# Expert groups of a two-layer trunk: two announced blocks per group, a down product in quarters, and VectorE and ScalarE in program order

## Chip, cores and metric

The kernel runs on one core of a Trainium2 chip. The metric is the device time of one execution in microseconds (us). Before the change three runs took 1015.21, 1004.9 and 1011.58 us; the median is 1011.58 us.

## What is computed

Two layers of a decoder trunk on 256 tokens of width 1024. Each layer has a token mixer, a cross-attention and a mixture of experts, with a layer norm behind each. The change lies in the experts alone:

```python
g_idx = jnp.argmax(g_logits, axis=-1)                      # one of 8 groups per token
e_logits = e_logits[jnp.arange(s), g_idx]
top_val, top_idx = lax.top_k(e_logits, TOP_K_IN_GROUP)     # 2 of the group's 4 experts
top_w = jax.nn.softmax(top_val, axis=-1) * g_weight
...
hid = jax.nn.silu(jnp.einsum('sd,edf->sef', xs, w_gate)) * jnp.einsum('sd,edf->sef', xs, w_up)
return jnp.einsum('sef,efd->sd', hid * gates[:, :, None], w_down)
```

There are 32 experts of inner width 256, so each layer reads 96 MB of expert weights. How many tokens an expert gets is known only when the router has run.

## The kernel before

**Groups.** `moe` (one call per layer) serves the eight groups one after the other, in the order of `SERVED`: 0 to 7 in the first layer, 1, 3, 0, 2, 4, 5, 6, 7 in the second. `expert(g)` (line 1405) computes a group. The four experts of the group stand side by side in the 128 columns or rows of TensorE, 32 tokens each: one matmul per expert, with 32 stationary columns.

**The straight path** of a group handles the first 32 tokens of each expert. In this order: the gate product (`up_to(b, 0, xg, wg)`, 8 steps k of four matmuls each, 256 columns), `silu` on ScalarE, the second half of the down product's way back of the group before (`late_back`), the up product (`up_to(b, 1, xg, wu)`), `act` on VectorE (the product of both), then the gather of the next group's tokens into `xg` by two `gather_half` (8 matmuls each into one bank; half 0 is evicted by VectorE, half 1 by ScalarE, four instructions each, through `affine`, line 460 or 462), then `dispatch(g, 32)`, the selection matrix of the second block, and `turned` (two transposes and an eviction by ScalarE, line 427).

**Blocks.** Tokens beyond 32 go in blocks of 32 through `over` (line 1366): `If(rv > 32 * c)`, with the next block's test nested in it, for c from 1 to 7. `rv` is the group's largest count, read from `cnt` into a register at run time. A block (`whole`) gathers its own tokens into `xo`, does gate, up, turn and down with the same weights. The group in `SPREAD` (group 0, the third served of the second layer) does only gate and up in its nest (`part`), and the down products in a second nest (`rest`). Here two groups of the first layer (3 and 6) take block 1 and skip block 2; of the second layer, group 0 takes blocks 1 to 3 and skips block 4, and group 2 takes block 1 and skips block 2; all other groups skip block 1.

**Announcements.** `foresee(rv, n)` puts a register operation and a branch hint into TensorE's program and names a test that comes later. For block 1 it stands ahead of step `TELL` of the up product (3 in both layers, 6 or 8 in a layer's first group); for every block c from 2 on it stands in the block before, behind the first `rows` of its `down` (`between`), or at the start of the block in `part`.

**Down product.** `down` (line 1295): `rows(c, n)` multiplies the turned activations by the down weights, two steps f of four matmuls of 512 columns; ScalarE evicts them times the gate weight as the high part of `y` (line 1310), VectorE subtracts to get the low part (line 1311). `back(c, n, y)` brings the tokens back to their places with the matrix `dt` that `combine` made: four matmuls of 512 columns, added to `ff` by VectorE (line 1327). Both have two halves. Between them `begin(n)` reads the next group's count, makes its `dt` and gate weight (`combine`) and its selection matrix (`dispatch` into `dn`).

**Weights.** Each group's 12 weight tiles of 1 MB are loaded by SyncE's transfer queue in one fixed order, over tiles that `free` returns: the gate and up tiles behind the group's nest of blocks, the down tiles behind its straight down product. The queue runs ahead as far as tiles are free.

**Order.** The framework's scheduler orders each engine's instructions unless a `manual_schedule` names the engine. ScalarE is pinned to program order up to the nest of each group, VectorE only until the first group's nest (`pinned[1].close()`).

## Time and profile before

| | |
|---|---|
| runs | 1015.21, 1004.9, 1011.58 us; median 1011.58 us |
| profiled execution | 1013.67 us, its span 1011.9 us |
| TensorE busy | 923.1 us (91%), 7948 matmuls |
| VectorE busy | 503.3 us (50%) |
| ScalarE busy | 340.9 us (34%) |
| transfers | 272.59 MB, mean 269 GB/s |
| weights' queue (q1) | 68.2% of the span |

The expert stage of the first layer takes about 270 to 512 us, that of the second 758 to 1000 us. The shares above are means over stages with different limits, so the stages are read one by one in the rows below. A row of the chain, of waits or of the timeline names an engine, a line, and tiles as `out<-in`; "PEq", "ACTq" or "DVEq" is the engine's instruction stream itself (a branch, a register, a semaphore), and L1368 stands for the `If`. The matmuls of a step overlap (four of them run side by side in the row groups of TensorE), so a duration times a count is more than the busy time.

### The profile page before, as it was taken

How to read it: one execution, taken by the hardware profiler on the slowest of the kernel's cores; microseconds unless marked ns; L12 is line 12 of the kernel's file. 1: busy time of each engine (PE TensorE's matmuls, PEld its weight loads, DVE VectorE, ACT ScalarE, POOL GpSimd, SP SyncE). 2: the span in 40 equal slices, each digit the busy share in tenths (PEclk: the TensorE clock that was granted, in tenths of full speed). 3: DMA queues.
4: the chain of work that ended last, by engine and by line, in shares of the span. 5: the costliest groups of instructions: out<-in, count | busy, mean ns of one | idle time of the engine just before them, and what ended most of it. 6: DMA issues, size and time to landing. Idle time of an engine off the chain costs nothing. (4 is left out here: it accounts for less than half of the span.)

```text
span 1011.9 us, 19936 instructions
## 1 busy us (share of the span) xinstructions
PE 923.1 (91%) x7948; PEld 688.2 (68%) x7948; DVE 503.3 (50%) x1258; ACT 340.9 (34%) x736; POOL 0.2 (0%) x4
## 2 busy tenths in 40 slices
PE   7899999999998688989899999999999888997885
PEld 7888987898754354856368899789885564444541
DVE  5755755544653333323466575554465414644434
ACT  5454855343411121011144475435442121121111
POOL 0000000000000000000000000000000000000000
PEclk9999999999999899999999999999999999999998
DMA  9842334538769988999786244553784994719995
GB/s 351 343 147 99 134 128 161 209 125 331 293 268 422 424 348 367 424 425 420 250 336 229 108 147 180 174 208 110 288 351 196 421 387 183 318 58 421 422 363 203
DMA packets 43774, 272.59 MB, mean 269 GB/s; under 512 B 4832, under 2 KB 5344, under 8 KB 13280
## 3 DMA queue, kind: packets, MB, share of 16 engines
q1 hardware_dynamic: 43472, 270.26, 68.2%
q8 instruction: 86, 1.41, 0.5%
q14 instruction: 72, 0.59, 0.2%
q10 hardware_dynamic: 144, 0.33, 0.1%
HBM read 269.52 MB, written 1.05 MB: 267 GB/s over the span
## 5 line engine op out<-in xcount | busy, mean ns | idle before, releaser
L432 DVE SCALAR_TENSOR_TENSOR wl<-main,wh 128x1024 fp32r<-128x1024 f32 (+1 forms) x93 | 112.2, 1211 | 112.1 <-ACT wh L431 111.9
L431 ACT ACTIVATE wh<-main 128x1024 fp32r<-128x1024 f32 (+1 forms) x93 | 97.3, 1052 | 116.5 <-PE bank L438 68.3
L437 PE MATMUL bank<-xh,wh 128*128 128x256 f32 x368 | 108.8, 298 | 5.6 <-ACT xh L488 3.6
L438 PE MATMUL bank<-xl,wh 128*128 128x256 f32 x368 | 105.8, 288 | 1.0 <-DVE xl L432 0.6
L439 PE MATMUL bank<-xh,wl 128*128 128x256 f32 x368 | 104.9, 286 | 0.0
L1277 PE MATMUL bank<-ext,xg 128*32 128x256 f32 x912 | 88.2, 392 | 2.9 <-DMA ext<-exp 2.8
L1327 DVE TENSOR_TENSOR ff<-ff,bank 128x512 f32<-128x512 f32 x84 | 53.2, 681 | 49.9 <-PE bank L1322 49.9
L437 PEld LDWEIGHTS bank<-xh,wh 128*128 128x128 f32 x368 | 71.1, 194 | 7.0 <-ACT xh L488 4.1
L438 PEld LDWEIGHTS bank<-xl,wh 128*128 128x128 f32 x368 | 71.3, 194 | 2.2 <-DVE xl L432 0.9
L439 PEld LDWEIGHTS bank<-xh,wl 128*128 128x128 f32 x368 | 71.4, 194 | 0.1
L1277 PE MATMUL bank<-main,xg 128*32 128x256 f32 x640 | 66.1, 384 | 2.4 <-DMA main<-exp 2.4
L460 ACT ACTIVATE xg<-bank,prmb 128x128 f32<-128x128 f32 x64 | 24.0, 456 | 123.3 <-PE bank L1227 117.2
L1310 ACT ACTIVATE y<-bank,sm 128x512 fp32r<-128x512 f32 (+1 forms) x46 | 30.7, 669 | 103.5 <-PE bank L1306 76.1
L1322 PE MATMUL bank<-y,dt 128*128 128x512 f32 (+1 forms) x184 | 56.9, 422 | 7.9 <-DVE y L1311 7.2
L1306 PE MATMUL bank<-ext,dn 128*32 128x512 f32 (+1 forms) x212 | 46.6, 670 | 17.5 <-PEq L1368 6.8
L437 PE MATMUL bank<-wh,oh 128*128 128x512 f32 (+1 forms) x160 | 60.9, 380 | 0.0
L439 PE MATMUL bank<-wh,ol 128*128 128x512 f32 (+1 forms) x160 | 59.1, 369 | 0.0
L1322 PEld LDWEIGHTS bank<-y,dt 128*128 128x128 f32 x184 | 29.6, 188 | 43.2 <-ACT y L1310 16.4
L438 PE MATMUL bank<-wl,oh 128*128 128x512 f32 (+1 forms) x160 | 59.0, 369 | 0.0
L1277 PEld LDWEIGHTS bank<-ext,xg 128*32 128x32 f32 x912 | 42.6, 112 | 22.5 <-issue 4.7
L1227 PEld LDWEIGHTS bank<-dn,xhat 128*128 128x128 f32 x448 | 51.1, 192 | 5.8 <-issue 4.9
L1227 PE MATMUL bank<-dn,xhat 128*128 128x128 f32 x448 | 53.7, 278 | 0.0
(300 smaller groups left out, 2008.7 us busy)
## 6 DMA issues: line engine op xcount, KB each, us to landing
ext<-exp SPq DMA_DIRECT2D x75, 1024.0 KB, 16.6
main<-exp SPq DMA_DIRECT2D x54, 1024.0 KB, 12.8
main<-wsq SPq DMA_DIRECT2D x33, 1024.0 KB, 5.0
main<-win SPq DMA_DIRECT2D x22, 1024.0 KB, 6.8
M<-exp SPq DMA_DIRECT2D x17, 1024.0 KB, 15.0
VM<-exp SPq DMA_DIRECT2D x8, 1024.0 KB, 17.1
xx<-exp SPq DMA_DIRECT2D x7, 1024.0 KB, 14.0
M<-wsq SPq DMA_DIRECT2D x5, 1024.0 KB, 7.1
```

The costliest lines, as they stand in the source:

```text
L431: ACT.activation(hi, src, AF.Copy, scale=scale)
L432: DVE.scalar_tensor_tensor(lo, src, scale, hi.bitcast(F32), op0=ALU.mult, op1=ALU.subtract)
L437: PE.matmul(psum, lh, rh, start=first, stop=False, skip_group_check=True)
L438: PE.matmul(psum, lh, rl, start=False, stop=False, skip_group_check=True)
L439: PE.matmul(psum, ll, rh, start=False, stop=last, skip_group_check=True)
L460: ACT.activation(dst, src, AF.Identity, bias=b, scale=g)
L1227: PE.matmul(b[:, k * 128:(k + 1) * 128], xhat[:, t, c:c + 128], d[:, t], start=(t == 0 and k == 0), stop=(t == 1), skip_group_check=True)
L1277: PE.matmul(pg[m * i:m * i + m, which * S:(which + 1) * S], x[:, k, m * i:m * i + m], w[:, k], start=(k == 0), stop=(k == 7), skip_group_c ...
L1306: PE.matmul(b[m * i:m * i + m], ht[:, f * 128 + m * i:f * 128 + m * i + m], w[:, o:o + n], start=(f == 0), stop=(f == 1), skip_group_check ...
L1310: ACT.activation(hi, b, AF.Copy, scale=gate)
L1322: PE.matmul(bs[t], dt[:, t * 128:(t + 1) * 128], y[i], start=(i == 0 and not held), stop=(i == 1), skip_group_check=bool(held))
L1327: DVE.tensor_add(o, o, bs[t])
```

## The change

- `TELL` becomes (7, 14) in both layers. For the groups that are not a layer's first, the announcement of block 1 goes from step 3 of the up product to step 7 of the gate product; a layer's first group has it at step 6 of the up product (before: 6 in the first layer, behind the product in the second).
- Inside a nest only the test of block 2 is announced (`c == 1`). In `rest` the same. The program holds 33 announcements instead of 114.
- `rows` and `back` do their 512 columns in two pieces of 256, so a down product's matmuls double in number (TensorE's program has 16570 listed rows instead of 14811).
- The turn comes between the two gather halves and writes a tile of its own, `f2`; `f1` is one fixed tile, and in a block `combine` uses `dn` and stands ahead of the turn.
- VectorE and ScalarE keep program order in the whole of `expert`, the blocks and the down product included.

```diff
@@ -33,7 +33,7 @@
 
 SERVED = [(0, 1, 2, 3, 4, 5, 6, 7), (1, 3, 0, 2, 4, 5, 6, 7)]
 SPREAD = [(), (0,)]
-TELL = [(3, 6), (3, 8)]
+TELL = [(7, 14), (7, 14)]
 
 
 FIRST = [o[0] for o in SERVED]
@@ -1101,7 +1101,7 @@
         xg = one(pz, "xg", [128, 8, 128])
         hs = tiles(pz, "hs", 2, [128, S])
         dn = one(pz, "dn", [128, S])
-        f1 = Arena(tiles(pz, "f1", 2, [128, S]))
+        f1, f2 = tiles(pz, "f1", 2, [128, S])
         dts = tiles(pz, "dt", 2, [128, S], F32R)
         ys = Arena([tiles(pz, "y", 2, [128, 512], F32R) for _ in range(2)])
         kc, grow = (dead[:, 0:2], dead[:, 2:4]) if late else (R[:, 6:8], prma[:, 0:2 * S].rearrange("p (i c) -> p i c", i=2))
@@ -1110,9 +1110,7 @@
 
         def g1():
 
-            t = f1.get()
-            f1.put(t)
-            return t
+            return f1
 
         def keep(t):
 
@@ -1255,9 +1253,9 @@
                 ACT.activation(grow[:, j], b[:, S:2 * S], AF.Copy)
                 banks.put(b)
 
-        def combine(base, o):
-
-            a, w = g1(), tiny(2)
+        def combine(base, o, a=None):
+
+            a, w = g1() if a is None else a, tiny(2)
             for j in range(2):
                 src = kc[:, j]
                 if j:
@@ -1300,11 +1298,12 @@
             def rows(c, n):
                 bank = banks.get()
                 b = bank[:, 0:n]
-                for f in range(2):
-                    for i, w in enumerate(ws):
-                        o = (c // n) * 2 * n + f * n
-                        PE.matmul(b[m * i:m * i + m], ht[:, f * 128 + m * i:f * 128 + m * i + m],
-                                  w[:, o:o + n], start=(f == 0), stop=(f == 1), skip_group_check=True)
+                for q in range(0, n, 256):
+                    for f in range(2):
+                        for i, w in enumerate(ws):
+                            o = (c // n) * 2 * n + f * n + q
+                            PE.matmul(b[m * i:m * i + m, q:q + 256], ht[:, f * 128 + m * i:f * 128 + m * i + m],
+                                      w[:, o:o + 256], start=(f == 0), stop=(f == 1), skip_group_check=True)
                 y = ys.get()
                 hi, lo = [v[:, 0:n] for v in y]
                 ACT.activation(hi, b, AF.Copy, scale=gate)
@@ -1319,8 +1318,9 @@
                 bs = [b[:, c % 512:c % 512 + n] for b in pair]
                 for i in range(2):
                     for t in range(2):
-                        PE.matmul(bs[t], dt[:, t * 128:(t + 1) * 128], y[i], start=(i == 0 and not held), stop=(i == 1),
-                                  skip_group_check=bool(held))
+                        for q in range(0, n, 256):
+                            PE.matmul(bs[t][:, q:q + 256], dt[:, t * 128:(t + 1) * 128], y[i][:, q:q + 256],
+                                      start=(i == 0 and q == 0 and not held), stop=(i == 1), skip_group_check=True)
                 if not held:
                     for t in range(2):
                         o = ff[:, t, c:c + n]
@@ -1367,7 +1367,7 @@
 
             with tc.If(rv > 32 * c, label=label):
                 nxt = []
-                f(c, lambda: nxt.append(foresee(rv, 32 * c + 32)) if c < top else None)
+                f(c, lambda: nxt.append(foresee(rv, 32 * c + 32)) if c == 1 else None)
                 if c < top:
                     over(rv, f, c + 1, *nxt, top=top)
 
@@ -1408,7 +1408,13 @@
             wg, wu, wd = [weights(g, i) for i in range(3)]
             with tc.manual_schedule(engines={mybir.EngineType.Activation}):
                 b = banks.get()
-                up_to(b, 0, xg, wg)
+                label, at = [], TELL[late][g == first]
+
+                def tell(k):
+                    if k == at:
+                        label.append(foresee(full[g], 32))
+
+                up_to(b, 0, xg, wg, tell=lambda k: g == first or tell(k))
                 silu(hs[0], b)
                 if n is None:
                     functions("natural_log_exp_and_others")
@@ -1416,21 +1422,16 @@
                     begin(g)
                 while late_back:
                     late_back.pop(0)()
-                label, at = [], TELL[late][g == first]
-
-                def tell(k):
-                    if k == at:
-                        label.append(foresee(full[g], 32))
-
-                up_to(b, 1, xg, wu, tell=tell)
-                tell(8)
+                up_to(b, 1, xg, wu, tell=lambda k: tell(8 + k))
+                tell(16)
                 act(hs[0], b)
                 banks.put(b)
                 if n is not None:
-                    for h in range(2):
-                        gather_half(xg, dn.rearrange("p (t c) -> p t c", t=2), h)
+                    gather_half(xg, dn.rearrange("p (t c) -> p t c", t=2), 0)
+                turned(hs[0], f2)
+                if n is not None:
+                    gather_half(xg, dn.rearrange("p (t c) -> p t c", t=2), 1)
                 d1 = dispatch(g, 32)
-                turned(hs[0], dn)
 
                 def hidden(c, h):
                     gather(xo, dispatch(g, 32 * c) if c > 1 else d1)
@@ -1447,7 +1448,8 @@
                     hidden(c, hs[1])
                     if n is None:
                         functions("natural_log_exp_and_others")
-                    down(g, turned(hs[1], g1()), combine(base(g) + 32 * c, other), wd, between=hint)
+                    back_way = combine(base(g) + 32 * c, other, dn)
+                    down(g, turned(hs[1], g1()), back_way, wd, between=hint)
 
                 def part(c, hint):
                     if c > 3:
@@ -1457,24 +1459,26 @@
                         hidden(c, hw[c])
 
                 def rest(c, hint):
-                    down(g, turned(hw[c], g1()), combine(base(g) + 32 * c, other), wd, between=hint)
+                    back_way = combine(base(g) + 32 * c, other, dn)
+                    down(g, turned(hw[c], g1()), back_way, wd, between=hint)
 
                 with apart():
                     over(full[g], part if wide else whole, label=label[0])
             free(g, 0, 8)
-            pinned[1].close()
             if wide:
                 with apart():
                     over(full[g], rest, top=3)
             if n is None:
                 last.extend([banks.get() for _ in range(2)])
-                down(g, dn, ways[g], wd, last=last)
+                down(g, f2, ways[g], wd, last=last)
             else:
-                down(g, dn, ways[g], wd, ahead=lambda: begin(n), put_off=late_back)
+                down(g, f2, ways[g], wd, ahead=lambda: begin(n), put_off=late_back)
             free(g, 8, 12)
 
+        pinned[1].close()
         for g in served:
-            expert(g)
+            with tc.manual_schedule(engines={mybir.EngineType.DVE, mybir.EngineType.Activation}):
+                expert(g)
             if l + 1 < depth and g == KEYS - 3:
                 reclaim(keys)
             if l + 1 < depth and g == KEYS:
```

Three places in the listed order of instructions. The first is on TensorE, the end of a straight path (second group of the first layer): `ext` and `xx` are up weights, L1227 or L1225 the gather's matmuls, L1290 or L1288 the transposes of the turn. Before:

```order
L1277 MATMUL bank_0_61<-ext_2_2262,xg_0_2244 32x256
L1277 MATMUL bank_0_61<-xx_0_69,xg_0_2244 32x256
L1227 MATMUL bank_3_64<-dn_0_2247,xhat_0_77 128x128 x8
L1227 MATMUL bank_7_68<-dn_0_2247,xhat_0_77 128x128 x8
L1290 MATMUL bank_6_67<-cst_0_70,hs_0_2245 128x128 x2
L1368 COMPARE_AND_BRANCH
```

and of the change:

```order
L1275 MATMUL bank_0_61<-ext_2_2262,xg_0_2244 32x256
L1275 MATMUL bank_0_61<-xx_0_69,xg_0_2244 32x256
L1225 MATMUL bank_3_64<-dn_0_2247,xhat_0_77 128x128 x8
L1288 MATMUL bank_7_68<-cst_0_70,hs_0_2245 128x128 x2
L1225 MATMUL bank_6_67<-dn_0_2247,xhat_0_77 128x128 x8
L1368 COMPARE_AND_BRANCH
```

The transposes moved ahead of the second gather half. The second place is on ScalarE, from the high parts of `y` of the group before to the same branch (L1281 or L1279 is `silu`, L460 the four evictions of the gather's second half, L427 the copy of the turn). Before:

```order
L1310 ACTIVATE y_0_2252<-bank_7_68,sm_14_92 128x512
L274 UNCONDITIONAL_BRANCH x4
L1310 ACTIVATE y_0_2254<-bank_6_67,sm_14_92 128x512
L1281 ACTIVATE hs_0_2245<-bank_0_61 128x256
L460 ACTIVATE xg_0_2244<-bank_7_68,prmb_0_73 128x128 x4
L427 ACTIVATE dn_0_2247<-bank_6_67 128x256
L1397 TENSOR_LOAD cnt_0_117
L1368 COMPARE_AND_BRANCH
```

and of the change:

```order
L1309 ACTIVATE y_0_2252<-bank_7_68,sm_14_92 128x512
L274 UNCONDITIONAL_BRANCH x4
L1309 ACTIVATE y_0_2254<-bank_6_67,sm_14_92 128x512
L1279 ACTIVATE hs_0_2245<-bank_0_61 128x256
L427 ACTIVATE f_43_1_2249<-bank_7_68 128x256
L460 ACTIVATE xg_0_2244<-bank_6_67,prmb_0_73 128x128 x4
L1397 TENSOR_LOAD cnt_0_117
L1368 COMPARE_AND_BRANCH
```

The copy of the turn moved ahead of the four evictions. The third place is on VectorE, the straight down product of the same stretch (`R` and `prma` hold the places and gate weights that `combine` reads, `dt` is its matrix, `dn` the next group's selection, `f` with `sm_6` the dispatch of block 1). Before:

```order
L1266 TENSOR_SCALAR dt_1_2251<-R_0_76 128x256
L1267 SCALAR_TENSOR_TENSOR f_43_1_2249,sm_5_83<-R_0_76,prma_0_72 128x256
L1264 SCALAR_TENSOR_TENSOR dt_1_2251<-R_0_76,dt_1_2251 128x256
L1267 SCALAR_TENSOR_TENSOR f_43_1_2249,sm_5_83<-R_0_76,prma_0_72 128x256
L1218 TENSOR_SCALAR f_43_0_2248<-cst_0_70,sm_6_84 128x128
L1269 TENSOR_TENSOR sm_5_83<-sm_5_83 128x1
L1218 TENSOR_SCALAR f_43_0_2248<-cst_0_70,sm_6_84 128x128
L1219 SCALAR_TENSOR_TENSOR f_43_0_2248<-cst_0_70,sm_6_84,f_43_0_2248 128x128 x2
L1216 TENSOR_SCALAR sm_21_99<-keyg_0_115 128x4
L1311 SCALAR_TENSOR_TENSOR y_1_2253<-bank_7_68,sm_14_92,y_0_2252 128x512
```

and of the change, from the low part of `y` on, and at the end of the straight path:

```order
L1310 SCALAR_TENSOR_TENSOR y_1_2253<-bank_7_68,sm_14_92,y_0_2252 128x512
L274 UNCONDITIONAL_BRANCH x4
L1310 SCALAR_TENSOR_TENSOR y_1_2255<-bank_6_67,sm_14_92,y_0_2254 128x512
L1397 TENSOR_LOAD cnt_0_117
L1264 TENSOR_SCALAR dt_1_2251<-R_0_76 128x256
...
L462 TENSOR_SCALAR xg_0_2244<-bank_3_64,prmb_0_73 128x128 x4
L1214 TENSOR_SCALAR sm_6_84<-keyg_0_115 128x4
L1216 TENSOR_SCALAR f_43_0_2248<-cst_0_70,sm_6_84 128x128
L1217 SCALAR_TENSOR_TENSOR f_43_0_2248<-cst_0_70,sm_6_84,f_43_0_2248 128x128
L1216 TENSOR_SCALAR f_43_0_2248<-cst_0_70,sm_6_84 128x128
L1217 SCALAR_TENSOR_TENSOR f_43_0_2248<-cst_0_70,sm_6_84,f_43_0_2248 128x128
L1368 COMPARE_AND_BRANCH
```

Both low parts of `y` now stand ahead of `combine`, and the dispatch of block 1 moved from there to the place right ahead of the branch.

## Rows read from the trace of the kernel before

**Rows 1.** By stretch: us, busy of five engines, TensorE clock, transfer share, GB/s.

```profile
286.00:373.00 87.00, 71.29 (x776) 40.06 (x780) 30.80 (x93) 13.60 (x33) 0.00 (x0) 0.94 1.00 416
...
381.30:480.00 98.70, 91.02 (x854) 62.03 (x858) 33.41 (x96) 12.49 (x29) 0.00 (x0) 0.97 1.00 416
...
771.10:832.50 61.40, 54.59 (x692) 34.74 (x696) 22.54 (x68) 11.36 (x28) 0.00 (x0) 1.00 0.99 410
832.50:847.60 15.10, 13.05 (x199) 8.51 (x188) 2.88 (x10) 1.89 (x5) 0.00 (x0) 1.00 0.03 13
...
868.00:905.50 37.50, 35.36 (x407) 20.24 (x406) 17.27 (x48) 7.18 (x16) 0.00 (x0) 1.00 0.32 127
905.50:993.00 87.50, 73.52 (x784) 38.09 (x784) 35.61 (x102) 14.03 (x29) 0.00 (x0) 0.98 0.97 388
```

**Rows 2.** Timeline of SyncE's queue, four issues: start us, us, engine, line, out<-in.

```profile
381.27 0.33 SPq L275 DMA_DIRECT2D ext<-exp  x1
...
490.14 0.33 SPq L275 DMA_DIRECT2D xx<-exp  x1
...
847.68 1.01 SPq L275 DMA_DIRECT2D main<-exp  x2
...
905.55 0.33 SPq L275 DMA_DIRECT2D ext<-exp  x1
```

**Rows 3.** Chain that ended last, first and last transfer of its end: start, us.

```profile
912.46 20.29 DMA main<-exp
...
985.96 6.99 DMA VM<-exp
```

**Rows 4.** TensorE's waits, 270–512, then 758–1000 us: total us, times, longest.

```profile
PE bank L1306 <- PEq L1368: 11.5, 5, 4.0
PE bank L1306 <- ACTq L1368: 5.0, 3, 1.7
...
PE bank L1322 <- DVE y L1311: 2.5, 4, 1.3
...
PE bank L1306 <- ACTq L1368: 6.7, 4, 1.7
PE bank L1322 <- DVE y L1311: 4.5, 5, 1.7
PE bank L1306 <- DMA main<-exp: 4.2, 1, 4.2
```

**Rows 5.** Timeline at the first group's turn, ScalarE and TensorE: start, us.

```profile
284.95 1.50 ACT L460 ACTIVATE xg<-bank,prmb 128x128 f32<-128x128 f32 x4 [6.52 <-PE bank L1227]
...
286.33 0.39 ACT L427 ACTIVATE dn<-bank 128x256 f32<-128x256 f32 x1
...
286.77 0.62 PE L1306 MATMUL bank<-M,dn 128*32 128x512 f32 x1 [1.71 <-ACTq L1368]
```

**Rows 6.** VectorE by line, 758–1000 us: count, busy us, mean ns, idle before.

```profile
L1219 DVE SCALAR_TENSOR_TENSOR f<-cst,sm,f 128x128 f32<-128x128 f32 x20 | 6.2, 344 | 0.1
...
L1218 DVE TENSOR_SCALAR f<-cst,sm 128x128 f32<-128x128 f32 x20 | 5.4, 281 | 0.1
```

**Rows 7.** Timeline of TensorE at two skips of block 2.

```profile
381.71 0.92 PE L1306 MATMUL bank<-main,dn 128*32 128x512 f32 x1 [3.48 <-PEq L1368]
...
899.40 1.06 PE L1306 MATMUL bank<-main,f 128*32 128x512 f32 x8 [0.47 <-ACT f L427]
...
905.97 0.64 PE L1306 MATMUL bank<-main,dn 128*32 128x512 f32 x4 [0.54 <-PEq L1368]
```

**Rows 8.** Timeline of TensorE behind the skip of block 4 (group 0).

```profile
848.40 0.41 PE L1290 MATMUL bank<-cst,prmb 128*128 128x128 f32 x2 [0.87 <-DVEq L1368]
```

**Rows 9.** Page, transfer queues: packets, MB, share of 16 engines.

```profile
q8 instruction: 86, 1.41, 0.5%
```

**Rows 10.** TensorE by form, 985–1000 us, last down product: busy us, mean ns.

```profile
L1306 PE MATMUL bank<-M,dn 128*32 128x512 f32 x4 | 2.1, 604 | 0.0
...
L1306 PE MATMUL bank<-M,dn 128*32 128x256 f32 x8 | 1.9, 382 | 0.0
```

## The prediction

> **What bounds the kernel now.** I read three views first: the table of busy time by stretch, the issues of the transfer queue, and the chain that ended last. The reader is to see in the first that the two expert stages are not one regime but three [rows 1]. In 286–373, 381–480, 771–832 and 905–993 us the 16 transfer engines are busy 97 to 100% of the time and move 388 to 416 GB/s: there the weights set the pace and TensorE waits inside a stream that it cannot hurry. In 832.5–847.6 transfers are nearly silent, a share of 0.03, and in 868–905.5 they are at 0.32: there TensorE sets the pace, because a group that takes a second block keeps its gate and up weights until its blocks are through. The queue shows when they come free [rows 2]: the next weights are asked for at 381.27, 490.14, 847.68 and 905.55 us, each time at the end of such a group's chain of blocks. After 905.55 the chain that ended last is transfers alone, from 912.46 to 985.96 + 6.99 = 992.95 us [rows 3], then a tail of the last down product and the norm. So an edit counts in full only if it moves one of those four releases; a TensorE wait elsewhere in a saturated stretch is covered.
>
> The waits of TensorE that the change aims at are real [rows 4]. In the first expert stage: 11.5 us behind its own branches (five waits), 5.0 us behind ScalarE's queue (three), 2.5 us behind the low part of y (four). In the second: 6.7 us behind ScalarE's queue (four), 4.5 us behind y (five), and one late branch of 4.2 us that the view puts down to a transfer. Together 34.4 us.
>
> **The change, part by part.** *Turning between the gather halves.* Now ScalarE runs four evictions of xg from 284.95 for 1.50 us and only then the 0.39 us copy of the turned activations, and TensorE waits 1.71 us for it [rows 5]. In the new order the turn stands ahead of the second half, and its copy ahead of the four evictions; 8 matmuls lie between, so the wait goes, seven times some 1.65 us (5.0 + 6.7 = 11.7). Each of the seven stands before or inside a stretch in which the transfers are at 97 to 100% [rows 1], so TensorE only arrives earlier at weights that aren't there yet. Worth to the end: 0.
>
> *VectorE in program order.* The low part of y now stands ahead of combine and dispatch, so 2.5 + 4.5 = 7.0 us of y waits go, again mostly in saturated stretches. Its price: the dispatch for block 1 (two comparisons of 281 ns, two combined ones of 344 ns [rows 6], 1.25 us, and a subtraction ahead) is now the last thing before the branch. A taken branch finds it less far ahead. The turn and the branch itself hide most of the 1.25 us; I take a third, 0.4 us, at each group that takes a block. There are two in each layer; those of the first layer are covered by the stretch they stand in, those of the second (groups 0 and 2) are not, since a block needs only weights that are already there. Bounds 0 and 1.25 each. Worth: +0.8.
>
> *Announcing in the gate product.* The announcement moves ahead of four matmuls of the gate product, the late back product and twelve matmuls of the up product, so the 11.5 + 4.2 us behind branches should shrink. One of them, 3.48 us at 381.71 [rows 7], is the test of block 2 inside a block; its announcement doesn't move, and the wait stays. The others lie in the saturated stretch 381–480 or after 905.55, where nothing of it shows at the end, save that the release at 490.14 could come earlier by what one of them costs, 11.5 / 5 = 2.3 us. Against that, the nested test before that release could come as late as the one at 381.71 does, against 0.54 us where such a test is in time (905.97, [rows 7]): 3.48 - 0.54 = 2.9. Bounds -2.3 and +2.9; I take 0, in the middle.
>
> *Leaving block 4 unnamed.* This is the term that decides. The third group served in the second layer takes blocks 1 to 3 and skips block 4. In the old kernel that skip is announced a whole block ahead, and the next matmul follows with 0.87 us idle [rows 8]. Unnamed, the code behind the skip has to come after the test. No row of before shows an unnamed skip, so I bound it: from below, nothing (the 0.87 us stays); from above by a test that was in time: its announcement stands behind the first row product of a block, which begins at 899.40, and the next work runs at 905.97 with only 0.54 us idle [rows 7], so whatever had to come took less than 905.97 - 899.40 - 0.54 = 6.0 us. Between them stands the late test at 381.71, 2.9 us above one in time. I take its **+2.9**: it is the one row of a skip whose code came late, and like this one it stands at the end of a chain of blocks. The whole of it moves 847.68, for in that stretch TensorE alone sets the pace (transfers at 0.03); TensorE's stretch to 905.5 then begins later by as much, and so do the transfers that end the kernel.
>
> [...]
>
> *Quarters.* A 256-column matmul of the down product is listed at 382 ns against 604 for 512 columns [rows 10], but the listed durations hold a fixed part that the next matmul overlaps. From below nothing; from above 2 x 382 - 604 = 160 ns on each of the 12 steps of a down product (four of the rows, eight of the back), 1.9 us. Six down products stand between 847.68 and the release at 905.55. I take near the lower end, 0.05 us each, +0.3, since the columns streamed are the same; above, at most 11 us.
>
> **Sum.** +2.9 (block 4) + 0.8 (dispatch) + 0.3 (quarters) + 0 (the turn, y, the announcements) = +4.0 us. The profiled execution has a span of 1011.9 us and took 1013.67 in all, so its like would take 1017.7; it stands 2.1 us above the median of the runs, 1011.58, and the median goes to **1015.5**.
>
> **Rivals.** *A, the waits reach the end (faster).* If the transfers only look saturated because TensorE frees tiles late, removed waits come through. All 34.4 us at once would give 981; half of them, less the 4.0, -13, so **998**. For it: TensorE is the busiest engine. Against it: transfers at 97 to 100% over the very stretches [rows 1], and a chain of transfers to 992.95 [rows 3]. It turns at 14 us coming through.
>
> *B, unnamed tests stall even where they go on (slower).* Blocks 2 to 3, and the second pass over the three parts, have tests without a name too. If each of three more stopped TensorE for 2.9 us, as the row at 381.71, the stretch up to 868 grows by 8.7 and the sum is +12.7, **1024**. Against it: such tests fall through into code that follows anyway. It decides from +10 us, four such stalls in all.
>
> *C, nothing comes of it.* The skip over block 4 costs nothing unnamed and all else is hidden: +0.8 + 0.3, **1012.7**. That would be so if the code behind the skip were already there.
>
> [...]
>
> **Chances.** Forecast 0.52, A 0.19, B 0.13, C 0.16. The forecast's own bounds are -2.3 + 0 + 0 + 0 and 2.9 + 6.0 + 2.5 + 11 = +22; with the quarters near their lower end, as I hold, +11.7, so its own range is 1009 to 1023. About 1%, 10 us, is what a measurement of this kernel can tell from no change: its three runs lie between 1004.9 and 1015.21. For 8 in 10 the range takes the forecast, C, the dearer end of A (0.09) and the cheaper end of B: **1000 to 1023**. Faster by over 1%: A, 0.18. Slower by over 1%: B and the forecast's upper end, 0.15. Within 1%: 0.67.
>
> **What would show it.** Right: TensorE's waits behind ScalarE's queue at the turn and behind y gone in both stages; the next weights after the three-block group asked for some 3 to 4 us later than 847.68 with a wait behind the branch ahead of the turned activations; and the stretch from the last release to the end as long as now. Wrong: releases at 381 or 490 that move by more than 3 us, transfer stretches that get shorter (A), or waits behind branches at several places of 802–868 (B). If the release at 847.68 does not move at all, the price of an unnamed skip was wrong (C).

## The result

The changed kernel takes 1015.07 us in the median of 17 runs (1012.49 to 1023.46), the kernel before 1011.53 us (1004.81 to 1015.4). The ratio is 1.0052, with a 95% interval of 1.0031 to 1.0073: slower by 3 to 7 us. The forecast was 1015.5 us. The number is right, and its working only in part: the term that was to decide measured 1.4 to 1.8 us where 2.9 were said, a term that the sum priced at 0.8 us is worth 4 to 7.5, and waits that were removed at a price of nothing do reach the end.

The profiled execution of the changed kernel has a span of 1015.0 us, 3.1 more than before. Its stretches, in the columns of [rows 1]:

```profile
286.00:373.00 87.00, 71.47 (x852) 45.41 (x848) 31.58 (x93) 13.12 (x30) 0.00 (x0) 0.92 1.00 419
381.30:480.00 98.70, 91.22 (x982) 68.56 (x974) 33.95 (x95) 12.72 (x30) 0.00 (x0) 0.98 1.01 419
...
832.50:847.60 15.10, 12.54 (x188) 8.23 (x180) 3.47 (x11) 1.89 (x5) 0.00 (x0) 1.00 0.02 5
...
905.50:993.00 87.50, 76.54 (x956) 49.33 (x954) 38.63 (x105) 14.54 (x30) 0.00 (x0) 0.96 0.96 380
```

The picture is that of before: full transfers where they were full, silence where they were silent. The four issues that [rows 2] followed, on SyncE's queue, now stand at

```profile
378.36 0.33 SPq L275 DMA_DIRECT2D ext<-exp  x1
...
486.20 0.33 SPq L275 DMA_DIRECT2D xx<-exp  x1
...
849.02 0.33 SPq L275 DMA_DIRECT2D main<-exp  x1
...
907.98 0.33 SPq L275 DMA_DIRECT2D ext<-exp  x1
```

that is 2.9 and 3.9 us earlier in the first layer and 1.3 and 2.4 us later in the second. These times have to be counted from the start of their stage, the first matmul of its gate product. Before, the two stages start at

```profile
272.81 0.42 PE L1277 MATMUL bank<-main,xg 128*32 128x256 f32 x4
...
757.81 0.64 PE L1277 MATMUL bank<-main,xg 128*32 128x256 f32 x8
```

and with the change at

```profile
270.33 0.42 PE L1275 MATMUL bank<-main,xg 128*32 128x256 f32 x4
...
756.76 0.85 PE L1275 MATMUL bank<-main,xg 128*32 128x256 f32 x12
```

The first stage began 2.5 us sooner, ahead of any changed instruction of the experts, and the second 1.05 us sooner. So 0.4 and 1.5 us of the earlier releases are the change's, and the later ones are 2.4 and 3.5 us late, not 1.3 and 2.4. To the last addition into `ff` the first stage takes 244.2 us where it took 243.3, the second 245.2 where it took 241.0: in these two executions most of the loss lies in the second layer. TensorE's waits, 270–512 and then 758–1000 us, in the columns of [rows 4]:

```profile
PE bank L1322 <- ACT y L1309: 6.1, 3, 3.0
...
PE bank L1305 <- PEq L1368: 3.6, 7, 0.9
PE bank L1345 <- DVEq L1368: 3.5, 1, 3.5
...
PE bank L1305 <- PEq L1368: 3.6, 6, 1.1
PE bank L1305 <- issue: 3.4, 2, 2.5
PE bank L1225 <- DVE f L1217: 3.3, 4, 1.4
PE bank L1288 <- DVE dt L1264: 2.6, 1, 2.6
...
PE bank L1322 <- issue: 2.5, 1, 2.5
PE bank L1305 <- DMA VM<-exp: 1.4, 1, 1.4
PE bank L1322 <- ACT y L1309: 1.7, 2, 1.3
```

Gone are the 11.7 us behind ScalarE's queue at the turn, and of the 11.5 us behind TensorE's own branches in the first layer 3.6 are left, none above 0.9. New are waits for `y` in the first layer (6.1 us in three, two of them of about 3), 2.5 us filed under "issue" at the same line in the second, 3.5 us at the first layer's end behind VectorE's stream, and, where 0.9 us stood before, 2.6 us behind the skip of block 4.

Where the 3 us waits come from is seen at the first of them, the skip of group 1 in the first layer (VectorE, ScalarE, TensorE by time):

```profile
301.01 0.35 DVE L1217 SCALAR_TENSOR_TENSOR f<-cst,sm,f 128x128 f32<-128x128 f32 x1
...
307.07 1.27 ACT L1309 ACTIVATE y<-bank,sm 128x512 fp32r<-128x512 f32 x2 [4.93 <-DVEq L1368]
307.79 0.75 DVE L1310 SCALAR_TENSOR_TENSOR y<-bank,sm,y 128x512 fp32r<-128x512 f32 x1 [6.43 <-ACT y L1309]
...
307.81 0.73 PE L1322 MATMUL bank<-y,dt 128*128 128x256 f32 x4 [3.01 <-ACT y L1309]
```

The records of VectorE's branch at this skip (the branch, and the first thing behind it; starts to a tenth of a us):

```profile
L1368 DVEq COMPARE_BRANCH  x1: 67/67/67, 301.0 to 301.0; - x1
L1368 DVEq EVENT_SEMAPHORE  x1: 21/21/21, 306.9 to 306.9; - x1
```

VectorE takes its branch at 301.0 us, with the last operation of the dispatch, and its stream goes on at 306.9. ScalarE, done with its own branch and work at 302.1, waits 4.93 us for that; TensorE has done both halves of the rows and waits 3.01 us for the first `y`. In the kernel before, TensorE waited here 1.65 us for the copy of the turn and 1.28 us for the low part of `y`, 2.9 us together. TensorE alone is told of a skip. With its two waits gone, VectorE's late stream is what ends last.

### The profile page after: what moved, and what is told of

Same layout as the page of the kernel before. It is cut to its first block, busy times and chain, and to the rows that moved or that the text cites. A ratio compares the mean times of both kernels' runs of the same rounds, so it can differ in the third digit from the quotient of the medians.

```text
span 1015.0 us, 21596 instructions
## 1 busy us (share of the span) xinstructions
PE 927.8 (91%) x8788; PEld 732.4 (72%) x8788; DVE 507.8 (50%) x1258; ACT 342.2 (34%) x736; POOL 0.2 (0%) x4
## 3 DMA queue, kind: packets, MB, share of 16 engines
HBM read 269.52 MB, written 1.05 MB: 267 GB/s over the span
## 5 line engine op out<-in xcount | busy, mean ns | idle before, releaser
L1310 DVE SCALAR_TENSOR_TENSOR y<-bank,sm,y 128x512 fp32r<-128x512 f32 (+1 forms) x46 | 33.0, 726 | 90.0 <-ACT y L1309 87.0
L1275 PE MATMUL bank<-main,xg 128*32 128x256 f32 x640 | 71.8, 413 | 4.1 <-DMA main<-exp 2.0
L1322 PEld LDWEIGHTS bank<-y,dt 128*128 128x128 f32 x352 | 47.7, 198 | 30.8 <-issue 15.0
L1305 PE MATMUL bank<-ext,f 128*32 128x256 f32 x560 | 61.5, 387 | 8.7 <-PEq L1368 3.6
L1322 PE MATMUL bank<-y,dt 128*128 128x256 f32 x352 | 59.0, 309 | 11.3 <-ACT y L1309 7.8
L1225 PEld LDWEIGHTS bank<-dn,xhat 128*128 128x128 f32 x448 | 52.2, 192 | 5.8 <-issue 4.9
L427 ACT ACTIVATE f<-bank 128x256 f32<-128x256 f32 x22 | 8.4, 384 | 141.3 <-PE bank L1288 134.5
```

What stands on the lines that cost most here:

```text
L1225: PE.matmul(b[:, k * 128:(k + 1) * 128], xhat[:, t, c:c + 128], d[:, t], start=(t == 0 and k == 0), stop=(t == 1), skip_group_check=True)
L1275: PE.matmul(pg[m * i:m * i + m, which * S:(which + 1) * S], x[:, k, m * i:m * i + m], w[:, k], start=(k == 0), stop=(k == 7), skip_group_c ...
L1305: PE.matmul(b[m * i:m * i + m, q:q + 256], ht[:, f * 128 + m * i:f * 128 + m * i + m], w[:, o:o + 256], start=(f == 0), stop=(f == 1), ski ...
L1310: DVE.scalar_tensor_tensor(lo, b, gate, hi.bitcast(F32), op0=ALU.mult, op1=ALU.subtract)
L1322: PE.matmul(bs[t][:, q:q + 256], dt[:, t * 128:(t + 1) * 128], y[i][:, q:q + 256], start=(i == 0 and q == 0 and not held), stop=(i == 1), ...
```

## Experiments

Four theories went in. Theory 1: the unnamed skip of block 4 costs. Theory 2: quarters make TensorE run out of instructions behind a skip. Theory 3: the place of the code decides which skip is late. Theory 4: the wait went over to VectorE, which reaches its branch later than before. Ratios are to the kernel before on the same chip, with 95% intervals; the changed kernel has 1.0052 (1.0031 to 1.0073).

**All tests named.**

```diff
-                f(c, lambda: nxt.append(foresee(rv, 32 * c + 32)) if c == 1 else None)
+                f(c, lambda: nxt.append(foresee(rv, 32 * c + 32)) if c < top else None)
```

> The changed kernel with every block's test announced again (block 4's too). Theory 1, the unnamed skip of block 4 is what costs: TensorE's wait behind that skip falls from 2.64 us to the 0.87 us of the kernel before, the weights behind group 0 are asked for some 2.5 us earlier counted from the second layer's first weights, and the time falls by 2.5 us, from 1015.1 to about 1012.6. Theory 2, the quarters make TensorE use up its instructions faster than they come after a skip: those waits (up to 3.5 us, in the rows behind a skip) stay, and the time stays within 1 us of 1015.

Ratio 1.0062 (1.0035 to 1.0088), median 1017.3 us: no gain. The wait behind block 4's skip did fall to 0.87 us, but the skip of block 2 in group 2, in time in the changed kernel, came 3.7 us late. Why is not shown; the 81 announcements more also move all code behind them:

```profile
PE bank L1305 <- PEq L1368: 6.1, 6, 3.7
```

**Halves again.** `rows` and `back` of the kernel before put back into the changed one.

```diff
-                for q in range(0, n, 256):
-                    for f in range(2):
+                for f in range(2):
...
-                                  w[:, o:o + 256], start=(f == 0), stop=(f == 1), skip_group_check=True)
+                                  w[:, o:o + n], start=(f == 0), stop=(f == 1), skip_group_check=True)
```

> The changed kernel with the 512-column pieces of the kernel before in rows and back. Theory 2: the six waits of 1.4 to 3.5 us inside and behind the rows go, those at the end of the first layer (3.47 us), behind group 2's skip (1.05) and in the tail (1.4) count, and the time falls by about 4 us to 1011. Theory 1: the quarters cost the 0.3 us of the forecast, so 1014.8.

Ratio 1.0079 (1.0051 to 1.0107), median 1020.5 us. Theory 2 falls as the main cause: the waits for `y` in the first layer stay with halves, and the time does not fall:

```profile
PE bank L1320 <- ACT y L1308: 5.3, 3, 2.8
```

**Both undone.** The two diffs above together.

> The changed kernel with both undone: every test announced and 512-column pieces; what is left of the change is the announcement in the gate product, the turn between the gather halves and the program order. Theories 1 and 2 together: 1015.1 - 2.5 - 4 = 1008.5, faster than both kernels. Theory 1 alone: 1012.3. Were the left parts without any worth, 1011.5.

Ratio 1.0029 (1.0006 to 1.0053), median 1014.4 us: still slower than before, with what was to be pure gain, the turn, the program order and the early announcement. So a part of the loss, at least, sits in these. The waits for `y` are there again:

```profile
PE bank L1320 <- ACT y L1308: 5.8, 2, 2.9
...
PE bank L1320 <- ACT y L1308: 4.0, 2, 3.2
```

**The kernel before, unnamed.**

```diff
-                f(c, lambda: nxt.append(foresee(rv, 32 * c + 32)) if c < top else None)
+                f(c, lambda: nxt.append(foresee(rv, 32 * c + 32)) if c == 1 else None)
```

> The kernel before with the tests of block 3 and on left without a name. Theory 1: the wait behind the skip of block 4 grows from 0.87 us by 1.8 to 2.9 us and the time by as much, 1011.5 to about 1014. Theory 2: with halves the code behind the skip arrives while TensorE still has work, the time stays at 1011.5.

Ratio 1.0073 (1.0047 to 1.0099), median 1019.5 us: about four times what the skip of block 4 explains. There the wait grew to 2.7 us, 1.8 more, as theory 1 says; but group 2's skip, named as before, came 3.4 us late here as well:

```profile
PE bank L1306 <- PEq L1368: 5.0, 2, 3.4
...
PE bank L1290 <- DVE dt L1266: 2.7, 1, 2.7
```

**Only the place of the code.** To the kernel before, transposes that never run were added in two blocks that no input reaches. What is executed stays the same; the code behind these blocks stands elsewhere, group 2's test among it. If theory 3 held there, the wait behind group 2's skip would go from 0.54 us to what the late one has, 3.48 [rows 7], and the time up by some 3 us.

```diff
+                def whole(c, hint):
+                    block(c, hint)
+                    if c == 7 and (late, g) in PAD:
+                        spare = banks.get()
+                        for _ in range(PAD[late, g]):
+                            PE.transpose(spare[:, 0:128], hs[1][:, 0:128], ident)
+                        banks.put(spare)
```

> The kernel before with never-run transposes added in two blocks that no input reaches (72 pairs behind block 7 of group 0 of the second layer, 56 behind block 7 of group 2). [...] Theory 1 (unnamed skips alone cost) and theory 2 (quarters alone): no change, within 1 us.

Ratio 0.9993 (0.9971 to 1.0015), median 1010.2 us: nothing. Group 2's skip stayed in time, and so, in this execution, was the skip of block 2 in the first layer, which stood 3.48 us late in the profile of before with the same code at the same place:

```profile
378.26 0.59 PE L1309 MATMUL bank<-main,dn 128*32 128x512 f32 x1 [0.55 <-PEq L1371]
...
901.58 0.64 PE L1309 MATMUL bank<-main,dn 128*32 128x512 f32 x4 [0.55 <-PEq L1371]
```

Theory 3 is not borne out by this shift; no other was run. Whether a named skip is late also changes from one execution to another with nothing changed near it; what decides it stays open.

**Block 4 alone named.** One announcement more in the changed kernel, two instructions.

```diff
-                f(c, lambda: nxt.append(foresee(rv, 32 * c + 32)) if c == 1 else None)
+                f(c, lambda: nxt.append(foresee(rv, 32 * c + 32)) if c == 1 or (f.__name__ == 'part' and c == 3) else None)
```

> The changed kernel with one announcement more, that of block 4 in group 0 of the second layer (two instructions, so nearly nothing else moves). Theory 1: TensorE's wait behind that skip falls from 2.64 us to 0.87 us and the time by 1.8 us, from 1015.1 to 1013.3. Theory 3: the same at that place, and nothing else. If the skip's price were hidden, 1015.1.

Ratio 1.0023 (1.0000 to 1.0046), median 1014.7 us. The wait falls from 2.6 to 1.2 us. The ratio falls by 0.29 points, but its own uncertainty (0.23 and 0.21 together some 0.31) covers that.

```profile
PE bank L1288 <- DVEq L1368: 1.2, 1, 1.2
```

**Dispatch of block 1 earlier.** The five VectorE operations go from right ahead of the branch to ahead of the product with the gate.

```diff
+                d1 = dispatch(g, 32)
                 act(hs[0], b)
...
-                d1 = dispatch(g, 32)
```

> The changed kernel with the dispatch of block 1 (five VectorE operations, 1.3 us) moved from the place right ahead of the branch to ahead of the product with the gate. VectorE then reaches its branch 1.3 us earlier. Theory 4, the wait moved from TensorE's branch to VectorE's: VectorE and ScalarE are not told of the skip, so their code comes some 5 us after VectorE reaches the branch, and TensorE stands 2.5 to 3.5 us for y behind its own skip: each of these waits falls by about 1.3 us, and the time by 1 to 2 us where no transfer covers them (the first layer's end, the tail), to about 1013.5. If the waits come from TensorE's own code instead, they stay as long, and the time stays at 1015.

Ratio 0.9978 (0.9955 to 1.0002), median 1011.1 us: 0.74 points below the changed kernel, and the two intervals do not meet. At the skip shown above, with the same columns:

```profile
299.71 1.36 DVE L462 TENSOR_SCALAR xg<-bank,prmb 128x128 f32<-128x128 f32 x4 [1.46 <-PE bank L1225]
...
305.29 0.69 ACT L1309 ACTIVATE y<-bank,sm 128x512 fp32r<-128x512 f32 x1 [2.07 <-DVEq L1368]
306.01 0.75 DVE L1310 SCALAR_TENSOR_TENSOR y<-bank,sm,y 128x512 fp32r<-128x512 f32 x1 [4.94 <-ACT y L1309]
...
306.03 0.74 PE L1322 MATMUL bank<-y,dt 128*128 128x256 f32 x4
```

and VectorE's branch:

```profile
L1368 DVEq COMPARE_BRANCH  x1: 67/67/67, 299.7 to 299.7; - x1
L1368 DVEq EVENT_SEMAPHORE  x1: 21/21/21, 305.2 to 305.2; - x1
```

ScalarE waits 2.07 us for VectorE instead of 4.93, and TensorE does not wait. The branch still takes 5.5 us to get through, but it is taken at 299.7 us, as the first of the four evictions starts (299.71) and while they run. In the changed kernel it came 2.4 us behind that start (298.63 to 301.0): there the branch stands behind the dispatch, whose five operations start one after the other from 299.91 to 301.01 us:

```profile
299.91 0.15 DVE L1214 TENSOR_SCALAR sm<-keyg 128x4 f32<-128x4 f32 x1
...
301.01 0.35 DVE L1217 SCALAR_TENSOR_TENSOR f<-cst,sm,f 128x128 f32<-128x128 f32 x1
```

So it moved by 2.4 us at this skip and not by 1.3, which is most of the 2.86 us that ScalarE's wait fell. Theory 4 holds on where the wait sits and on what moves it; its size was too small.

**All three engines told.**

```diff
-            tc.mark_branch_hint_location(label, rv > n, engines=[mybir.EngineType.PE])
+            tc.mark_branch_hint_location(label, rv > n, engines=[mybir.EngineType.PE, mybir.EngineType.DVE, mybir.EngineType.Activation])
```

> The changed kernel with every announcement made to VectorE and ScalarE too, at the same places. Theory 4: the waits for y behind a skip (3.01, 2.85, 3.47, 2.45 us) fall under 1 us, VectorE's stop at its branch falls from some 6 us to under 2, and the time falls by 3 to 5 us to 1010 to 1012. If the transfers cover them: under 1 us of difference, 1015, though the waits go.

Ratio 1.0081 (1.0052 to 1.0110), median 1020.7 us: not faster, and the waits for `y` are more, not fewer:

```profile
PE bank L1322 <- ACT y L1309: 10.2, 5, 3.3
```

In the first layer that is 10.2 us in five where the changed kernel has 6.1 in three. An announcement on VectorE and ScalarE at these places does not bring what it brings on TensorE, 1.4 us at the skip of block 4 above. By the records of VectorE's branch its stream goes on 5 us or more behind it at 8 of the 12 skips of block 1, against 5 in the changed kernel. Why stays open.

**Both edits.** Dispatch earlier and block 4 named.

> The changed kernel with the dispatch of block 1 ahead of the product with the gate and block 4's test announced, the two edits together. If the two prices found one by one add up (the early dispatch took 0.74% off, the name of block 4 0.29%), the time falls from 1015.1 by about 10 us less what they share, to 1006 to 1009, below the kernel before (1010.5 to 1011.5). If block 4's name is worth only what stands behind the skip, 1.8 us: 1009.3. If they share their gain: 1011.

Ratio 0.9983 (0.9958 to 1.0007), median 1008.4 us. No sum of the two gains is seen: beside the early dispatch alone (0.9978) the name brings nothing that can be measured (uncertainty 0.35 points), though the wait behind the skip falls from 3.1 to 1.3 us:

```profile
PE bank L1288 <- PEq L1368: 1.3, 1, 1.3
```

**Dispatch twice.** The suspected cost doubled.

```diff
                 d1 = dispatch(g, 32)
+                d1 = dispatch(g, 32)
```

> The changed kernel with the dispatch of block 1 computed twice right ahead of the branch (the second writes the same values). Theory 4, what VectorE does between its last eviction and its branch delays the code behind the skip: VectorE reaches the branch 1.3 us later, its stops of some 5.5 us there stay, TensorE's waits for y behind a skip grow by up to 1.3 us each, and the time by 1 to 3 us to 1016 to 1018. Theory 5, the dispatch's cost is only its own 0.4 us at the two groups with blocks: 1015.9. If VectorE's stops depend on where its code lies, some of them vanish and others come.

Ratio 1.0283 (1.0243 to 1.0323), median 1040.7 us: 23 points in a thousand more than with one, some 23 to 25 us for five operations of 1.3 us in 16 groups, 21 us if they all stood bare on the path. Every theory had said 3 us at most. The waits for `y` came where they had been and where they hadn't (both layers):

```profile
PE bank L1322 <- ACT y L1309: 16.4, 4, 4.2
...
PE bank L1322 <- ACT y L1309: 12.1, 4, 4.2
```

28.5 us in eight waits, some 18 more than the 10.3 of the changed kernel (6.1 + 1.7 + 2.5). Two things in the traces go with it. VectorE's stream goes on 5 us or more behind its branch at 10 of the 12 skips of block 1, where the changed kernel has 5: what changed is not only 1.3 us in front of each branch, but how many branches are late. And TensorE's clock is lower: the runs have a median granted clock of 0.959, those of the changed kernel 0.976, and 85.7 us of the profiled execution are at a granted clock of 0.50 instead of 55.8. What each of the two costs is not separated.

The full transfer queue hid little of this. From the second layer's first issue to the release behind group 0 it is 86.7 us at a share of 0.71, where [rows 1] of before have 76.5 us at (61.4 x 0.99 + 15.1 x 0.03) / 76.5 = 0.80, some 61 us of transfers in both: the stretch is 10 us longer, and its end is set by TensorE's chain, not by the queue.

```profile
783.80:870.50 86.70, 69.64 (x948) 47.77 (x939) 29.90 (x93) 12.83 (x32) 0.00 (x0) 0.96 0.71 293
```

**Early dispatch, all named, halves.**

> The changed kernel with the early dispatch, every test announced and 512-column pieces; beside the run with early dispatch and block 4 named it shows what quarters do when the two prices are taken out. Theory 2 (quarters cost instructions behind a skip): faster than that run by 1 to 3 us, about 1006. Forecast's term (quarters cost 0.3 us): the same within 1 us. Against the run with every test named and halves (1014.4): 4 us faster, 1010.5, if the dispatch's place is worth the same there.

Ratio 0.9966 (0.9941 to 0.9991), median 1007.5 us: faster than both kernels, by 3.4 us than the kernel before. The waits for `y` are down to 0.9 us in its first layer; what is left there is transfers and 3.9 us of branches, none above 1.2:

```profile
PE bank L1275 <- DMA ext<-exp: 5.0, 4, 1.9
PE bank L1304 <- PEq L1366: 3.9, 7, 1.2
...
PE bank L1320 <- ACT y L1308: 0.9, 2, 0.5
```

Beside the run with every test named and halves but the dispatch late (1.0029) the dispatch's place is worth 0.63 points, beside block 4's pair (1.0023 to 0.9983) 0.40, and alone 0.74: three pairs, 4 to 7.5 us.

**Quarters alone**, in the kernel before.

> The kernel before with rows and back in pieces of 256 columns and nothing else. The forecast's term: +0.3 us, 1011 to 1012, and at most +11. Theory 2: waits inside the rows behind a skip appear as in the changed kernel, +2 to +4 us, 1013 to 1015.

Ratio 1.0019 (0.9993 to 1.0046), median 1012.1 us. Within its uncertainty no change, on the side of a small loss. In the first layer the list has waits at the rows filed under "issue", which [rows 4]'s view of before doesn't show for that layer:

```profile
PE bank L1307 <- issue: 5.0, 3, 3.0
```

Theory 2 has its waits, but no price for them is seen; the interval leaves room for up to 4.7 us.

**Stage by stage.** One profiled execution of each kernel, from the first matmul of a stage's gate product to its last addition into `ff`, and the time in it for which TensorE's granted clock was 0.50 (us):

| kernel | first stage | at clock 0.50 | second stage | at clock 0.50 |
|---|---|---|---|---|
| before | 243.3 | 20.5 | 241.0 | 3.4 |
| before, never-run code added | 240.9 | 13.7 | 241.2 | 3.4 |
| before, quarters | 241.9 | 13.7 | 240.8 | 10.2 |
| changed | 244.2 | 20.5 | 245.2 | 10.2 |
| early dispatch | 236.3 | 6.8 | 246.3 | 20.5 |
| block 4 named | 243.7 | 17.1 | 245.5 | 13.7 |
| block 4 named, early dispatch | 236.4 | 10.2 | 242.7 | 13.7 |
| all named, halves | 242.2 | 23.9 | 244.0 | 6.8 |
| all named, halves, early dispatch | 234.7 | 10.2 | 243.2 | 17.1 |
| dispatch twice | 256.7 | 34.1 | 257.7 | 23.9 |

The early dispatch takes 7.9, 7.3 and 7.5 us off the first stage in its three pairs, and changes the second by +1.1, -2.8 and -0.8. The first three rows show how far one execution can be trusted: they lie within 2.4 us of each other in the first stage and within 0.4 in the second.

Beside the shorter waits the clock has a part in the first stage's gain. In the changed kernel it falls to 0.50 behind the wait of 3.01 us shown above; with the early dispatch, from the same place of the program, it does not (last columns as in [rows 1]; the changed kernel, then the early dispatch):

```profile
309.35:312.76 3.41, 3.41 (x36) 1.70 (x40) 3.30 (x13) 0.00 (x0) 0.00 (x0) 0.50 1.01 423
...
306.03:319.50 13.47, 8.91 (x98) 4.99 (x102) 7.72 (x22) 1.07 (x2) 0.00 (x0) 1.00 1.01 420
```

So the wait of 3.01 us was followed by 3.41 us at a clock of 0.50, and both are gone with the early dispatch. How the 7.3 to 7.9 us divide between waits and clock, no run separates.

## Why the prediction came out as it did

- **What bounds the kernel: half right, and one of the two steps that failed.** The four releases exist, and the one behind block 4 came later as forecast. That "the weights set the pace" where the transfer share is 0.97 to 1.00 did not hold for TensorE. The largest waits for weights in the kernel before, of the first stage and (a late branch of 4.2 us apart, which the view puts down to a transfer) of the second, are these:

```profile
PE bank L1277 <- DMA xx<-exp: 3.1, 2, 1.9
...
PE bank L1277 <- DMA main<-exp: 0.8, 2, 0.6
```

  In all such waits come to 9.3 us in the first stage and 1.3 in the second. Full transfers do not show that TensorE waits for them; and a tile freed later is a transfer started later. The kernel in which the turn's, `y`'s and VectorE's waits are nearly all out is 3.4 us faster than before, with a first stage of 234.7 us against 240.9 to 243.3.
- **Turn between the halves: mechanism right.** The 11.7 us of waits went in full. What the turn alone is worth no run shows; together with the program order and the early announcement, each priced at nothing but for the dispatch, it is worth 3.4 us once the dispatch is out of the way (0.9966, with halves and all tests named as before).
- **VectorE in program order: right place, wrong size, and the other step that failed.** "I take a third, 0.4 us, at each group that takes a block" looked at groups with blocks. The cost lies at the groups that skip: there VectorE comes to its branch only behind the dispatch, ScalarE and TensorE wait for what it does behind it, and taking the dispatch out of that place is worth 4 to 7.5 us in three pairs of kernels (each with an uncertainty of some 0.35 points), nearly all of it in the first stage, against the 0.8 of the sum. The row was there: in the kernel before, at the same skip of group 1, VectorE stood idle for 4.74 us behind its branch, while TensorE waited 1.65 us for ScalarE and 1.28 for the low part of `y`:

```profile
308.84 0.29 DVE L1266 TENSOR_SCALAR dt<-R 128x256 fp32r<-128x256 f32 x1 [4.74 <-DVEq L1368]
```

  Taking TensorE's two waits away left VectorE's as the last to end, and the dispatch in front of the branch made it later.
- **Announcing in the gate product: right that the branches would be in time** (3.6 us left of 11.5), wrong that 381.71 would keep its 3.48 us. It was in time here, at 0.62 us, and also in an execution of the kernel before with padding; its lateness is not a property of the program alone.
- **Leaving block 4 unnamed: mechanism right, size too large.** The wait behind the skip is 2.6 to 3.1 us in the six kernels without the name and 0.9 to 1.3 in those with it: in five pairs that differ in names alone 1.4 to 1.8 us of price, not the 2.9 of the sum. The release behind it came 2.4 us later, counted from the stage's start, where 3 to 4 were forecast. On the whole time the name alone was worth 0.29 points with an uncertainty of 0.31, and nothing that could be measured beside the early dispatch. "This is the term that decides" was not borne out. That the code behind an unnamed skip comes after the test agrees with the trace: TensorE's branch there lasts 0.37 us in the kernel before and 3.39 in the changed one, and a packet of the instruction queue (the queue of [rows 9]) starts within the second, 1.0 us behind the branch's start, and none within the first. How much of the 3.39 us the packet accounts for is not shown.

```profile
L1368 PEldq COMPARE_BRANCH  x1: 367/367/367, 846.1 to 846.1; - x1
...
L1368 PEldq COMPARE_BRANCH  x1: 3387/3387/3387, 845.5 to 845.5; - x1
```

- **Quarters: not contradicted.** +0.3 us was forecast (for six down products; the trace has five in that stretch, which changes nothing at 0.05 us each). Measured is a ratio of 1.0019 with an interval that holds 1, and the sign changes from pair to pair (halves for quarters: slower by 0.27 points with block tests unnamed, faster by 0.33 with all named, each with some 0.35 of uncertainty).
- **Rivals.** A was right on the mechanism and wrong on its price: waits taken away do reach the end, by 3.4 us in the fastest kernel here. B's stalls did not come at the tests that fall through: TensorE's branch takes 0.07 to 0.08 us at these in the changed kernel. C's free skip did not come either: the 1.4 to 1.8 us are there in all five pairs. That the total is right is in part luck: in the first stage two errors of some 7 us, the gain from the removed waits (243.3 to 236.3) and the cost of the dispatch's place (236.3 to 244.2), cancel to +0.9 us. In the second the loss of 4.2 us stands where the forecast had its 4.0, at the releases behind groups 0 and 2, but the skip is 1.8 of it; the other 2.4 are not taken apart, and the stage has 6.8 us more at a clock of 0.50 than before.

## What to carry to other kernels

When a late engine is made early, ask which engine ends last at the same join, and what the edit puts ahead of that engine's own branch: five small operations put in front of VectorE's branch, which most groups never use, cost 4 to 7.5 us here. A full transfer queue is no proof that a wait beside it is covered: look at how long the engine waits for the transfers (1.3 us in a stage of 241 here), or add a delay. Look at the clock of a stretch too: here it stood at 0.50 for 3.41 us behind a wait of 3.01 us. And when code carries many data-dependent skips, undo one part at a time and look at every skip in the trace before believing the total.

## What the runs showed that had not been expected

- How often VectorE is late behind a skip goes with the kernel: its stream goes on 5.1 to 7.3 us behind its branch at 8 of the 12 skips of block 1 in the kernel before and its three variants, at 5 in the changed kernel and seven of its variants, at 8 with all engines told and at 10 with the dispatch twice; at the other skips it is 0.5 to 3.4 us. What decides which of them are late was not settled.
- Doubling 1.3 us of work in front of VectorE's branch raised the time by 2.3 points in a hundred (1.0052 to 1.0283); taking it away lowered it by 0.74. The response is far from proportional; the number of late branches and the clock go with it.
- Announcing the same skips to VectorE and ScalarE made the kernel no faster (1.0081).
- The same named skip at the same place in the same code was 3.48 us late on TensorE in one execution and in time, at 0.55 us, in another.
- Between runs of one kernel, time and granted clock go together: the kernel before took 1006.47 us at a mean clock of 0.984 and 1018.23 us at 0.973.
- Transposes that never run (72 and 56 pairs) in two blocks changed nothing (0.9993), while removing 81 announcements cost 0.73 points in the kernel before. In that trace 1.8 us stand behind the skip of block 4 and 2.9 us more than before behind group 2's late skip; the rest stays open.
